# Seven-product pairs ordered by PSUM banks, a plain first part of six tiles, and features combined on VectorE

## The chip, the cores and the metric

The kernel runs on one core of a Trainium2 chip. The metric is the device time of one execution in microseconds (us). Comparisons use the median of several executions; the profile shows a single one. In the text PE is TensorE (matmuls), ACT is ScalarE, DVE is VectorE, POOL is GpSimd, and SP is the engine whose queue issues the loads of the weights.

## The reference

The kernel computes two layers of a hybrid decoder trunk on a sequence of 512 positions with 1024 features, all in float32. A layer is a feed-forward network (FFN), a mixer and a second FFN:

```python
def swiglu(h, w_gate, w_up, w_down):
    return (jax.nn.silu(h @ w_gate) * (h @ w_up)) @ w_down

for l in range(DEPTH):                                    # DEPTH = 2
    x = x + 0.5 * swiglu(rms_norm(x, ffn1_norm[l]), ffn1_w_gate[l], ffn1_w_up[l], ffn1_w_down[l])
    h = rms_norm(x, mix_norm[l])
    a, g, q, k, v = jnp.split(h @ w_in[l], splits, axis=-1)
    conv_out = conv_module(a, g, ...)                     # causal depthwise convolution, width 31
    diff_out = diff_attention(q, k, v, ...)               # 4 heads, two softmax maps each
    x = x + jnp.concatenate([conv_out, diff_out], axis=-1) @ w_out[l]
    x = x + 0.5 * swiglu(rms_norm(x, ffn2_norm[l]), ffn2_w_gate[l], ffn2_w_up[l], ffn2_w_down[l])
```

The hidden width of an FFN, D_FF, is 2816: 22 tiles of 128. There are four FFNs in all, and the change touches only them.

## The kernel before

**Layout.** Everything is kept transposed, with features on the 128 partitions and the 512 positions along the free dimension. `x` is 8 tiles of 128 x 512.

**Splitting.** A matmul operand in float32 is split into two operands of the type float32r: a high part (`hi`, a copy made by ACT) and a low part (`lo`, the remainder, subtracted by DVE). This is `parts_of`, lines 96 and 97. A product of two such operands takes three matmuls (high x high, high x low, low x high: `mm3`, lines 156, 159 and 160). `chunk` loads 128 x 1024 weights by a DMA on SP into a buffer of the ring `wraw` (6 buffers) and splits them into the rings `whi` and `wlo` (4 buffers each). `gather` (line 108) does the same for blocks of the down weights, and `whi2`, `wlo2` (2 buffers of 512) hold one more half tile.

**An FFN.** `ffn` runs over the 22 hidden tiles in three parts, `PARTS`, of 8, 8 and 6. In a part, each hidden tile is a *pair*: the gate product and the up product, 128 x 512 each, in two PSUM banks that `pair_banks` takes in turn from three tags (sc, po, mm). `gated` then splits silu(gate) * up into `hh` (ACT, line 374) and `hl` (DVE, line 375). When the tiles of a part are there, the down product runs: 8 output tiles, each a chain over the tiles of the part in a bank of the tag mm (`ps_d`), added to `x` by DVE (line 417).

**Plain pairs.** The first three pairs of an FFN (`PLAIN` = 3) are multiplied plainly, 2 x 8 x 3 = 48 matmuls of 512 columns. They use `x` times the gain, without the factor 1/rms, which is applied to their results. `first_products` makes the first two and the norm `r` (the tile `rb`) beside them.

**Seven-product pairs.** All later pairs use a scheme that has 7 products where 8 are usual: the input is cut in 2 x 2 blocks (first and second half of the features, first and second half of the positions), the weights in gate and up by halves of the features. The seven block products are 4 x 3 matmuls of 256 columns each, 84 in all. They need sums of weights (`sums`, line 123: two loads on SP, four additions on POOL, lines 136 to 140, and six splits) and combined features. `Halves` makes the latter once per FFN: `hn` is the normalised input (DVE, line 300), `ht` holds three differences of blocks (POOL, lines 303 and 304, and DVE, lines 305 and 306), which are split into `th` and `tl` (lines 307 and 308). `settle` then overwrites `acth` and `actl`, which the plain pairs read, with the split `hn` (lines 313 and 314).

**The order within a pair.** `seven` (line 323) accumulates in four half banks: a and d in the first bank, b and c in the second. A half bank that is wanted later in two places is copied by ACT to the tiles `g` and `n`. The framework takes a whole bank as the unit of waiting: PE does not write a bank while ACT or DVE reads it.

```python
go(a, "g1", "b11", first=True)
S.activation(g[:, :HS], a, AF.Copy)
go(c, "u2u1", "t1", first=True)
S.activation(n[:, HS:], c, AF.Copy)
go(b, "g2", "b21")
go(a, "g1u2u1", "t2")
S.activation(g[:, HS:], a, AF.Copy)
go(d, "u2", "t4")
...
go(a, "g1u1", "t3")
```

**What sets the order on the engines.** Each engine works its queue in order. The queues are filled by a scheduler that runs the program in a timeline of its own and gives each engine, of the instructions that are ready, the one that comes first in the program. The first matmul of each block product is pinned to the program's order. So matmuls of a down product may be put ahead of the last products of a part, and sums and splits of later weights run ahead as far as the rings have free buffers.

Of the kernel before, what the change touches and what calls it, by code (L numbers as in the profile page):

```python
# [37 lines left out]
MASK = -1e30  # L38
RLEN = 640
STATS_AT = 5  # L40

PLAIN = 3

PARTS = ((0, 8), (8, 8), (16, 6))
HS = SEQ // 2

SPACE = 392

# [18 lines left out]
def trunk(ctx: ExitStack, tc: tile.TileContext, xt, par, lamv, relb, onehot,  # L67
          gu1, dn1, wag, wqkv, wout, gu2, dn2, out):
    nc = tc.nc
    V, S, G, T = nc.vector, nc.scalar, nc.gpsimd, nc.tensor  # L70
# [4 lines left out]
    wp = ctx.enter_context(tc.tile_pool(name="wp", bufs=1))  # L75
# [78 lines left out]
    def mm3(ps, w, x, start, stop, pin=False):  # L154
        (wh, wl), (xh, xl) = w, x
        first = T.matmul(ps, wh, xh, start=start, stop=False)  # L156
# [29 lines left out]
    def col(l, name, i=0):  # L186
        c = _AT[name] + i
        return pars[l][:, c : c + 1]
# [91 lines left out]
    def pair_banks(turn):  # L280
        tag = ("sc", "po", "mm")[turn % 3]
        return [bank(tag, "ps_pair") for _ in range(2)]


    class Halves:
# [4 lines left out]
        def __init__(self, fp, pr, r):  # L290
            self.th = fp.tile([P, 3, KT // 2, HS], F32R, tag="th", name="th")
            self.tl = fp.tile([P, 3, KT // 2, HS], F32R, tag="tl", name="tl")

            self.whole = []
            free = [f"hh{n}" for n in range(PLAIN, 8)] + [f"hl{n}" for n in range(PLAIN, 6)]
            a, b = slice(0, HS), slice(HS, SEQ)
            for j in range(KT // 2):
                ha, hb = (fp.tile([P, SEQ], F32, tag=free[i], name="hn") for i in (2 * j, 2 * j + 1))
                for k, h in ((j, ha), (j + KT // 2, hb)):
                    V.scalar_tensor_tensor(h, x[:, k, :], col(pr.l, pr.gain, k), r, op0=ALU.mult, op1=ALU.mult)  # L300
                    self.whole.append((k, h))
                t = fp.tile([P, 3 + j % 2, HS], F32, tag=("ht", "hl6")[j % 2], name="ht")[:, :3]
                G.tensor_tensor(t[:, 1], hb[:, b], ha[:, b], op=ALU.subtract)
                G.tensor_tensor(ha[:, b], ha[:, a], ha[:, b], op=ALU.subtract)
                V.scalar_tensor_tensor(t[:, 0], ha[:, b], -1.0, hb[:, b], op0=ALU.mult, op1=ALU.subtract)
                V.scalar_tensor_tensor(t[:, 2], t[:, 0], -1.0, hb[:, a], op0=ALU.mult, op1=ALU.subtract)
                S.activation(self.th[:, :, j, :], t, AF.Copy)
                V.tensor_tensor(self.tl[:, :, j, :], t, f32(self.th[:, :, j, :]), op=ALU.subtract)
# [11 lines left out]
            k0, c = {"b11": (0, 0), "t1": (0, HS), "b21": (KT // 2, 0), "b22": (KT // 2, HS)}[name]  # L320
            return lambda j: (acth[:, k0 + j, c : c + HS], actl[:, k0 + j, c : c + HS])

    def seven(halves, w, banks, fp):

        a, d = banks[0][:, :HS], banks[0][:, HS:]
        b, c = banks[1][:, :HS], banks[1][:, HS:]
        g = fp.tile([P, SEQ], F32, tag="g", name="g", bufs=2)
        n = fp.tile([P, SEQ], F32, tag="n", name="n", bufs=2)

        def go(ps, wt, xt, first=False):  # L330


            at = halves.get(xt)
            for j in range(KT // 2):
                (wh, wl), (xh, xl) = wpart(w[wt], j), at(j)
                for i, (l, r) in enumerate(((wh, xh), (wh, xl), (wl, xh))):
                    mm = T.matmul(ps, l, r, start=first and i == j == 0, stop=False, skip_group_check=True)  # L337
                    if i == j == 0:
                        tc.keep_in_program_order(mm)

        go(a, "g1", "b11", first=True)
        S.activation(g[:, :HS], a, AF.Copy)
        go(c, "u2u1", "t1", first=True)
        S.activation(n[:, HS:], c, AF.Copy)  # L344
        go(b, "g2", "b21")
        go(a, "g1u2u1", "t2")
        S.activation(g[:, HS:], a, AF.Copy)  # L347
        go(d, "u2", "t4")
        S.activation(n[:, :HS], d, AF.Copy)
        go(c, "all", "b22")  # L350
        V.tensor_tensor(banks[1], banks[1], g, op=ALU.add)
        S.activation(g, banks[1], AF.Silu)
        go(a, "g1u1", "t3")
        V.tensor_tensor(d, a, n[:, HS:], op=ALU.add)
        V.tensor_tensor(a, a, n[:, :HS], op=ALU.add)
        V.scalar_tensor_tensor(banks[0], banks[0], -1.0, g, op0=ALU.mult, op1=ALU.mult)
        return banks[0]

    def ffn(pr, gu, dn, after, lead=None, aside=None):
        with tc.tile_pool(name="ffn", bufs=1) as fp:  # L360
            r = halves = None
            for m0, many in PARTS:
                hh, held, more = [], [], []

                def gated(n, us):
                    hi = fp.tile([P, SEQ], F32R, tag=f"hh{n}", name="hh")
                    if n < 6:
                        lo = fp.tile([P, SEQ], F32R, tag=f"hl{n}", name="hl")
                    elif n == 6:
                        two = fp.tile([P, 2, SEQ], F32R, tag="hl6", name="hl")  # L370
                        lo, more[:] = two[:, 0], [two[:, 1]]
                    else:
                        lo = more.pop()
                    S.activation(hi, us, AF.Copy)  # L374
                    V.tensor_tensor(lo, us, f32(hi), op=ALU.subtract)  # L375
                    hh.append((hi, lo))

                for mm in range(many):
                    m = m0 + mm
                    if m == 4 and aside:  # L380
                        aside()
                    if m >= PLAIN:
                        gated(mm, seven(halves, sums(gu[m, 0], gu[m, 1]), pair_banks(m), fp))
                        continue
                    w = lead if lead and m == 0 else [chunk(gu[m, 0]), chunk(gu[m, 1])]
                    held.append((mm, w, pair_banks(m)))
                    if m == 0:
                        continue
                    if m == 1:
                        _, _, r = first_products(pr, [h[1] for h in held], [h[2] for h in held])  # L390
                        halves = Halves(fp, pr, r)
                    else:
                        for k in range(KT):
                            for i in range(2):
                                mm3(held[-1][2][i], wpart(w[i], k), pr[k], k == 0, k == KT - 1)
                    if m == PLAIN - 1:
                        halves.settle()
                    for n, _, ps in held:
                        gs = fp.tile([P, SEQ], F32, tag="g", name="gs", bufs=2)
                        V.tensor_tensor(gs, ps[0], r, op=ALU.mult)  # L400
                        S.activation(gs, gs, AF.Silu)
                        us = fp.tile([P, SEQ], F32, tag="n", name="us", bufs=2)
                        V.tensor_tensor(us, ps[1], r, op=ALU.mult)
                        V.tensor_tensor(us, us, gs, op=ALU.mult)
# [363 lines left out]
    pr = Prep(0, "ffn1_norm")  # L768
# [7 lines left out]
    for l in range(DEPTH):  # L776
# [15 lines left out]
        pr = nxt["p"]  # L792
# [74 lines left out]
```

## Time and profile before

| | |
|---|---|
| time, median of 3 executions | 2130.51 us (2130.44 to 2132.23) |
| the profiled execution | 2129.2 us, of which its instructions span 2127.4 us |
| mean granted TensorE clock | 0.964 of full speed |
| busy: PE, weight loads, DVE, ACT, POOL | 87%, 76%, 63%, 44%, 39% of the span |
| HBM read | 172.74 MB, mean 83 GB/s over the span |

The page of the profile and the answers to questions on the trace give one execution. A row of a stretch lists, for each engine, its busy time and in brackets its instructions; then the granted clock, the mean busy share of the DMA engines and the rate. A row of waits says who waited for whom, then the sum in us, the times and the longest. A row of a group gives line, engine, operation, the written and read tiles with their shapes and the count, then the busy time, the mean of one in ns, and the idle time of the engine ahead of it with what ended it. A row of the timeline gives start, duration, and in square brackets the idle time before. Ends of matmuls are modelled, so a matmul's duration overlaps the next one; the distance of their starts is what one costs.

### The profile page before, as it was taken

The numbers are of one execution on the slowest core, as the hardware profiler recorded it, in microseconds if no ns is written. First come the engines' busy times: TensorE is split into PE (matmuls) and PEld (weight loads), VectorE is DVE, ScalarE is ACT, GpSimd is POOL, SyncE is SP. The second block draws the span as 40 slices with busy tenths as digits, with TensorE's granted clock in tenths as the row PEclk, the third lists the DMA queues.
The fourth block names the chain that finished last, engine by engine and source line by source line (L and its number), as shares of the span: only waits on it lengthen the run. The fifth ranks groups of instructions, "written<-read, shape, count | busy, mean of one in ns | idle before, by whom it ended". The sixth has DMA issues, their size and how long they took to land. (4 is left out here: it accounts for less than half of the span.)

```text
span 2127.4 us, 28881 instructions
## 1 busy us (share of the span) xinstructions
PE 1857.6 (87%) x11124; PEld 1625.7 (76%) x11124; DVE 1338.9 (63%) x1880; ACT 934.5 (44%) x1608; POOL 839.5 (39%) x576
## 2 busy tenths in 40 slices
PE   7589899899998598898986988989999958988988
PEld 5478788788787578878876788788887847788787
DVE  8655755558869655646576456465688686465463
ACT  5343533445745434424443334244458434244241
POOL 6313513139935414324044143240597452242330
PEclk9699999999999799999997999999999989999999
DMA  4232232332211131322411313224231213223131
GB/s 153 80 110 70 80 111 68 110 99 90 79 41 50 50 119 60 111 79 70 129 44 50 115 60 114 75 70 129 90 90 50 60 40 100 70 80 110 59 107 52
DMA packets 69017, 176.72 MB, mean 83 GB/s; under 512 B 8455, under 2 KB 26022, under 8 KB 68880
## 3 DMA queue, kind: packets, MB, share of 16 engines
q1 hardware_dynamic: 67104, 172.00, 25.3%
q0 software_dynamic: 1632, 2.81, 0.4%
q8 instruction: 87, 1.43, 0.3%
q14 instruction: 50, 0.41, 0.1%
q10 hardware_dynamic: 144, 0.08, 0.0%
HBM read 172.74 MB, written 3.42 MB: 83 GB/s over the span
## 5 line engine op out<-in xcount | busy, mean ns | idle before, releaser
L97 DVE TENSOR_TENSOR wlo<-wraw,whi 128x512 fp32r<-128x512 f32 (+1 forms) x582 | 612.2, 1082 | 283.5 <-ACT whi L96 281.0
L96 ACT ACTIVATE whi<-wraw 128x512 fp32r<-128x512 f32 (+1 forms) x626 | 478.1, 791 | 626.3 <-PE ps_pair L337 271.2
L136 POOL TENSOR_TENSOR wraw<-wraw 128x512 f32<-128x512 f32 x76 | 119.3, 1570 | 855.8 <-DMA wraw<-in_gu 544.2
L337 PE MATMUL ps_pair<-acth,whi 128*128 128x256 f32 x1216 | 356.1, 293 | 105.6 <-ACT acth L313 67.9
L337 PE MATMUL ps_pair<-actl,whi 128*128 128x256 f32 x1216 | 351.4, 289 | 13.6 <-DVE actl L314 13.6
L337 PE MATMUL ps_pair<-acth,wlo 128*128 128x256 f32 x1216 | 349.0, 287 | 0.4 <-DVE wlo L97 0.4
L337 PE MATMUL ps_pair<-th,whi 128*128 128x256 f32 x912 | 265.7, 292 | 93.9 <-ACT g L347 91.4
L337 PEld LDWEIGHTS ps_pair<-acth,whi 128*128 128x128 f32 x1216 | 237.6, 196 | 121.9 <-ACT acth L313 68.8
L156 PE MATMUL ps_d<-hh,whi 128*128 128x512 f32 x704 | 280.0, 401 | 31.8 <-ACT hh L374 29.9
L159 PE MATMUL ps_d<-hl,whi 128*128 128x512 f32 x704 | 280.7, 399 | 3.7 <-DVE hl L375 3.6
L160 PE MATMUL ps_d<-hh,wlo 128*128 128x512 f32 x704 | 280.5, 399 | 0.0
L337 PE MATMUL ps_pair<-tl,whi 128*128 128x256 f32 x912 | 259.1, 284 | 0.0
L337 PE MATMUL ps_pair<-th,wlo 128*128 128x256 f32 x912 | 258.8, 284 | 0.0
L337 PEld LDWEIGHTS ps_pair<-th,whi 128*128 128x128 f32 x912 | 175.5, 193 | 107.5 <-ACT g L347 104.2
L337 PEld LDWEIGHTS ps_pair<-actl,whi 128*128 128x128 f32 x1216 | 238.0, 196 | 18.6 <-DVE actl L314 17.8
L337 PEld LDWEIGHTS ps_pair<-acth,wlo 128*128 128x128 f32 x1216 | 238.2, 196 | 0.7 <-DVE wlo L97 0.7
L156 PEld LDWEIGHTS ps_d<-hh,whi 128*128 128x128 f32 x704 | 133.7, 191 | 66.6 <-ACT hh L374 32.4
L337 PEld LDWEIGHTS ps_pair<-tl,whi 128*128 128x128 f32 x912 | 176.0, 193 | 0.5
L337 PEld LDWEIGHTS ps_pair<-th,wlo 128*128 128x128 f32 x912 | 175.9, 193 | 0.0
L417 DVE SCALAR_TENSOR_TENSOR x<-ps_d,x 128x512 f32<-128x512 f32 x96 | 66.1, 690 | 168.5 <-PE ps_d L160 168.4
L159 PEld LDWEIGHTS ps_d<-hl,whi 128*128 128x128 f32 x704 | 135.8, 193 | 36.3 <-DVE hl L375 9.4
L160 PEld LDWEIGHTS ps_d<-hh,wlo 128*128 128x128 f32 x704 | 135.2, 192 | 31.0 <-DVE wlo L97 2.8
(177 smaller groups left out, 3325.7 us busy)
## 6 DMA issues: line engine op xcount, KB each, us to landing
wraw<-in_gu SPq DMA_DIRECT2D x174, 512.0 KB, 3.6
wraw<-in_wqkv SPq DMA_DIRECT2D x24, 512.0 KB, 3.6
wraw<-in_dn SPq DMA_DIRECT2D x52, 192.0 KB, 2.6
wraw<-in_wag SPq DMA_DIRECT2D x16, 512.0 KB, 3.5
wraw<-in_wout SPq DMA_DIRECT2D x16, 512.0 KB, 3.5
wraw<-in_dn SPq DMA_DIRECT2D x24, 320.0 KB, 3.2
wraw<-in_dn SPq DMA_DIRECT2D x28, 256.0 KB, 3.1
wraw<-in_dn SPq DMA_DIRECT2D x48, 128.0 KB, 3.3
```

Source lines behind the costliest of these rows:

```text
L96: S.activation(hi, raw, AF.Copy)
L97: (eng or V).tensor_tensor(out=lo, in0=raw, in1=f32(hi), op=ALU.subtract)
L136: G.tensor_tensor(two[:, h[1]], up[:, h[1]], up[:, h[0]], op=ALU.add)
L156: first = T.matmul(ps, wh, xh, start=start, stop=False)
L159: T.matmul(ps, wh, xl, start=False, stop=False)
L160: T.matmul(ps, wl, xh, start=False, stop=stop)
L337: mm = T.matmul(ps, l, r, start=first and i == j == 0, stop=False, skip_group_check=True)
L417: V.scalar_tensor_tensor(x[:, m, :], ps, 0.5, x[:, m, :], op0=ALU.mult, op1=ALU.add)
```

## The change

1. `PARTS` becomes 6, 8, 8 instead of 8, 8, 6, and `PLAIN` is the size of the first part: pairs 0 to 5 of each FFN are plain, 6 to 21 by seven products (before: 0 to 2 and 3 to 21). A plain pair finishes its gate product before its up product begins.
2. `Halves` is made after the first two pairs have been gated; both differences that POOL made are now made by DVE. Its `hn` tiles lie in `hh6`, `hh7`, `hl6`, `hl7` and the four buffers of `whi2` and `wlo2`. `settle` is called after the pairs of the first part, ahead of its down product.
3. `seven` has another order of products: c, d, [the last product of the pair before], a, b, c, a. Its own last product (g1 + u1 with t3) and the steps that follow it are returned as a function `rest`, which the next pair calls in its third place, or `finish` at the end of a part. In the last pair of a part, the fifth and sixth products change places. The copies go to one tile `keep` of four half rows; a and d are copied by one instruction.
4. The tiles `g` and `n` become one tile of the tag `gn`; the special case for `hl6` goes.

`sums` itself is the same in both kernels: its four additions were on POOL already.

```diff
-PLAIN = 3
-PARTS = ((0, 8), (8, 8), (16, 6))
+PARTS = ((0, 6), (6, 8), (14, 8))
+PLAIN = PARTS[0][1]
...
-            free = [f"hh{n}" for n in range(PLAIN, 8)] + [f"hl{n}" for n in range(PLAIN, 6)]
+            free = [(fp, tag, 1) for tag in ("hh6", "hh7", "hl6", "hl7")]
+            free += [(wp, tag, 2) for tag in ("whi2", "wlo2") for _ in range(2)]
...
-                G.tensor_tensor(t[:, 1], hb[:, b], ha[:, b], op=ALU.subtract)
-                G.tensor_tensor(ha[:, b], ha[:, a], ha[:, b], op=ALU.subtract)
+                V.tensor_tensor(t[:, 1], hb[:, b], ha[:, b], op=ALU.subtract)
+                V.tensor_tensor(ha[:, b], ha[:, a], ha[:, b], op=ALU.subtract)
...
-    def seven(halves, w, banks, fp):
+    def seven(halves, w, banks, fp, before, last):
...
-        go(a, "g1", "b11", first=True)
-        S.activation(g[:, :HS], a, AF.Copy)
         go(c, "u2u1", "t1", first=True)
-        S.activation(n[:, HS:], c, AF.Copy)
+        S.activation(keep[:, 3], c, AF.Copy)
+        go(d, "u2", "t4", first=True)
+        before()
+        go(a, "g1", "b11")
+        S.activation(keep[:, :2], banks[0].rearrange("p (n c) -> p n c", n=2), AF.Copy)
         go(b, "g2", "b21")
+        if not last:
+            go(c, "all", "b22")
         go(a, "g1u2u1", "t2")
-        S.activation(g[:, HS:], a, AF.Copy)
-        go(d, "u2", "t4")
-        S.activation(n[:, :HS], d, AF.Copy)
-        go(c, "all", "b22")
-        V.tensor_tensor(banks[1], banks[1], g, op=ALU.add)
-        S.activation(g, banks[1], AF.Silu)
-        go(a, "g1u1", "t3")
-        V.tensor_tensor(d, a, n[:, HS:], op=ALU.add)
-        V.tensor_tensor(a, a, n[:, :HS], op=ALU.add)
-        V.scalar_tensor_tensor(banks[0], banks[0], -1.0, g, op0=ALU.mult, op1=ALU.mult)
-        return banks[0]
+        S.activation(keep[:, 2], a, AF.Copy)
+        if last:
+            go(c, "all", "b22")
+        V.tensor_tensor(two, two, g, op=ALU.add)
+        S.activation(g, two, AF.Silu)
+
+        def rest():
+            go(a, "g1u1", "t3")
+            V.tensor_tensor(d, a, keep[:, 3], op=ALU.add)
+            V.tensor_tensor(a, a, keep[:, 1], op=ALU.add)
+            us = banks[0].rearrange("p (n c) -> p n c", n=2)
+            V.scalar_tensor_tensor(us, us, -1.0, g, op0=ALU.mult, op1=ALU.mult)
+            return banks[0]
+
+        return rest
...
+                def finish():
+                    if late:
+                        n, rest = late.pop()
+                        gated(n, rest())
...
                     if m >= PLAIN:
-                        gated(mm, seven(halves, sums(gu[m, 0], gu[m, 1]), pair_banks(m), fp))
+                        w = sums(gu[m, 0], gu[m, 1])
+                        late.append((mm, seven(halves, w, pair_banks(m), fp, finish, mm == many - 1)))
                         continue
...
-                        for k in range(KT):
-                            for i in range(2):
-                                mm3(held[-1][2][i], wpart(w[i], k), pr[k], k == 0, k == KT - 1)
-                    if m == PLAIN - 1:
-                        halves.settle()
+                        for i in range(2):
+                            products(pr, w, held[-1][2][i], i)
...
+                    if m == 1:
+                        halves = Halves(fp, pr, r)
+                finish()
+                if m0 == 0:
+                    halves.settle()
```

More of the change, by code (lines that the diff above doesn't have):

```diff
@@ L294, in __init__ @@
             self.whole = []
-            free = [f"hh{n}" for n in range(PLAIN, 8)] + [f"hl{n}" for n in range(PLAIN, 6)]
+            free = [(fp, tag, 1) for tag in ("hh6", "hh7", "hl6", "hl7")]
+            free += [(wp, tag, 2) for tag in ("whi2", "wlo2") for _ in range(2)]
             a, b = slice(0, HS), slice(HS, SEQ)
             for j in range(KT // 2):
-                ha, hb = (fp.tile([P, SEQ], F32, tag=free[i], name="hn") for i in (2 * j, 2 * j + 1))
-                for k, h in ((j, ha), (j + KT // 2, hb)):
+                for k in (j, j + KT // 2):
+                    pool, tag, bufs = free.pop()
+                    h = pool.tile([P, SEQ], F32, tag=tag, name="hn", bufs=bufs)
                     V.scalar_tensor_tensor(h, x[:, k, :], col(pr.l, pr.gain, k), r, op0=ALU.mult, op1=ALU.mult)
                     self.whole.append((k, h))
-                t = fp.tile([P, 3 + j % 2, HS], F32, tag=("ht", "hl6")[j % 2], name="ht")[:, :3]
-                G.tensor_tensor(t[:, 1], hb[:, b], ha[:, b], op=ALU.subtract)
-                G.tensor_tensor(ha[:, b], ha[:, a], ha[:, b], op=ALU.subtract)
+                (_, ha), (_, hb) = self.whole[-2:]
+                t = fp.tile([P, 3, HS], F32, tag="ht", name="ht", bufs=2)
+                V.tensor_tensor(t[:, 1], hb[:, b], ha[:, b], op=ALU.subtract)
+                V.tensor_tensor(ha[:, b], ha[:, a], ha[:, b], op=ALU.subtract)
                 V.scalar_tensor_tensor(t[:, 0], ha[:, b], -1.0, hb[:, b], op0=ALU.mult, op1=ALU.subtract)
@@ L321, in get @@
             return lambda j: (acth[:, k0 + j, c : c + HS], actl[:, k0 + j, c : c + HS])
-    def seven(halves, w, banks, fp):
+    def seven(halves, w, banks, fp, before, last):
         a, d = banks[0][:, :HS], banks[0][:, HS:]
         b, c = banks[1][:, :HS], banks[1][:, HS:]
-        g = fp.tile([P, SEQ], F32, tag="g", name="g", bufs=2)
-        n = fp.tile([P, SEQ], F32, tag="n", name="n", bufs=2)
+        two = banks[1].rearrange("p (n c) -> p n c", n=2)
+        keep = fp.tile([P, 4, HS], F32, tag="gn", name="keep", bufs=2)
+        g = keep[:, 0::2]
         def go(ps, wt, xt, first=False):
@@ L362, in ffn @@
             for m0, many in PARTS:
-                hh, held, more = [], [], []
+                hh, held, late = [], [], []
                 def gated(n, us):
                     hi = fp.tile([P, SEQ], F32R, tag=f"hh{n}", name="hh")
[L367 to L373, printed above, removed]
+                    lo = fp.tile([P, SEQ], F32R, tag=f"hl{n}", name="hl")
                     S.activation(hi, us, AF.Copy)
```

11 lines of the change are left out of this document (5 added, 6 removed).

## The prediction

> **What bounds the kernel now.** I read the page first, then the time by stretch, then who made TensorE (PE) wait, then the chain of waits and single instructions where it pointed.
>
> ```profile
> span 2127.4 us, 28881 instructions
> PE 1857.6 (87%) x11124; PEld 1625.7 (76%) x11124; DVE 1338.9 (63%) x1880; ACT 934.5 (44%) x1608; POOL 839.5 (39%) x576
> ```
>
> PE is the busiest. The stretches, with PE's instructions in brackets behind its busy time and the granted clock after POOL; those with a clock under 1 are the starts of the four feed-forward networks (FFN):
>
> ```profile
> core 0: us, PE busy (x) PEld busy (x) DVE busy (x) ACT busy (x) POOL busy (x), PEclk, DMA share, GB/s
> 629.00:648.00 19.00, 19.00 (x161) 19.00 (x160) 11.22 (x18) 8.15 (x14) 4.65 (x3) 1.00 0.18 58
> 1077.00:1084.00 7.00, 7.00 (x32) 5.79 (x32) 3.33 (x2) 1.25 (x2) 5.64 (x4) 1.00 0.26 75
> 46.40:158.80 112.40, 73.83 (x469) 66.51 (x467) 66.96 (x98) 45.93 (x80) 27.13 (x25) 0.80 0.28 90
> 685.30:782.40 97.10, 65.66 (x463) 60.52 (x462) 57.60 (x84) 42.78 (x75) 23.99 (x16) 0.88 0.24 76
> 1108.10:1205.90 97.80, 67.86 (x464) 62.70 (x462) 57.19 (x81) 40.37 (x71) 21.45 (x16) 0.86 0.24 76
> 1732.80:1829.90 97.10, 65.67 (x463) 60.51 (x462) 58.62 (x84) 42.79 (x75) 22.20 (x16) 0.88 0.24 76
> 1865.30:1975.40 110.10, 94.14 (x715) 89.04 (x714) 67.75 (x85) 51.14 (x93) 35.57 (x24) 1.00 0.29 92
> 1872.50:1947.50 75.00, 63.49 (x504) 61.05 (x504) 52.69 (x67) 38.43 (x73) 30.60 (x20) 1.00 0.30 99
> 2013.20:2095.40 82.20, 70.09 (x536) 66.60 (x534) 48.04 (x63) 38.31 (x69) 24.36 (x16) 1.00 0.24 78
> ```
>
> The first two rows are stretches in which PE never rests: 256-column matmuls start every 19.00/160 = 0.119 us, 512-column ones every 7.00/31 = 0.226. A pair by seven products (84 x 256) so needs 10.0 us, a plain pair (48 x 512) 10.85. The row 1872.50 holds exactly six seven-pairs (504 matmuls) in 75.0 us: 12.5 each, 2.5 lost per pair, at full clock. Who made PE wait:
>
> ```profile
> PE ps_pair L337 <- ACT g L347: 91.4, 63, 1.7
> PE ps_pair L337 <- ACT acth L313: 67.9, 4, 18.1
> PE ps_pair L337 <- ACT n L344: 35.7, 63, 6.1
> PE ps_d L156 <- ACT hh L374: 29.9, 12, 2.5
> ```
>
> The first and third are the copies out of a PSUM bank in which PE wants to go on; in the chain of waits they recur each 12.5 us, with a weight split ahead of the copy in ACT's queue:
>
> ```profile
> 1884.98 0.61 ACT whi L96
> 1885.92 7.46 PE ps_pair L337 x60
> 1893.84 3.02 PE ps_pair L337 x23
> 1897.48 0.61 ACT whi L96
> ```
>
> The second happens once per FFN. The timeline shows PE at a standstill for 18 us between the plain and the seven-product pairs, because the features (L304) stand in POOL's queue behind a sum of weights that waits for a load:
>
> ```profile
> 1743.92 3.57 POOL L136 TENSOR_TENSOR wraw<-wraw 128x512 f32<-128x512 f32 x1 [13.19 <-DMA wraw<-in_gu]
> 1753.38 1.40 POOL L304 TENSOR_TENSOR hn<-hn 128x256 f32<-128x256 f32 x2
> 1754.82 0.58 PE L337 MATMUL ps_pair<-acth,whi 128*128 128x256 f32 x1 [18.05 <-ACT acth L313]
> 1732.80:1761.00 28.20, 6.34 (x25) 4.82 (x24) 21.18 (x34) 12.71 (x21) 10.87 (x8) 0.58 0.07 19
> ```
>
> In the last row 25 matmuls (3 us) take 28.2 us, at a mean clock of 0.58.
>
> **The lost time, stage by stage.** A first part holds 5 seven-pairs (420 x 256) and 42 early down matmuls: 50.0 + 9.5 = 59.5 us. It took 97.1, 97.8 and 97.1: 37.6, 38.3 and 37.6 lost; 112.4 in the first FFN, 52.9 lost (it also prepares the bias). The second part (672 x 256, 42 x 512: 89.5) took 110.1: 20.6 lost; the third (504, 30: 66.8) took 82.2: 15.4. I take these two for all four FFNs. In all 166.4 + 82.4 + 61.6 = 310.4 us. Without it the kernel would take 2127.4 - 310.4 = 1817.0.
>
> **Plain part of six.** Twelve pairs go from seven-product to plain: 12 x 0.85 = +10.2 us of PE, so 1827.2 is the floor. Their loads on SP stay two of 512 KB a pair; 48 sums leave POOL. The down weights are still 22 gathers an FFN (6, 8, 8 instead of 8, 8, 6), on SP ahead of the loads for pair 6.
>
> **Halves and settle.** Features can now be made under pairs 2 to 5 (43.4 us of PE), and `settle` (8 copies on ACT, 8 subtractions on DVE) runs under the first down product, 144 x 0.226 = 32.5 us. So the 28 us hole should go, and the low clock with it. What comes late next is DVE:
>
> ```profile
> 1721.00:1733.00 12.00, 12.00 (x54) 9.78 (x53) 11.99 (x13) 4.49 (x7) 6.87 (x6) 1.00 0.15 44
> 1724.63 7.31 DVE L300 SCALAR_TENSOR_TENSOR hn<-x,par,rb 128x512 f32<-128x512 f32 x8
> L308 DVE TENSOR_TENSOR tl<-ht,th 128x768 fp32r<-128x768 f32 x16 | 16.7, 1056 | 0.7 <-ACT th L307 0.6
> 1829.17 1.22 DVE L97 TENSOR_TENSOR wlo<-wraw,whi 128x1024 fp32r<-128x1024 f32 x1
> ```
>
> DVE is full when the norm becomes known. From there to the end of pair 5 it has features: 7.3 + 4 x (1.06 + 4 x 0.43, 256-wide steps as in the row of L355 below) = 18.4, of which the two steps taken from POOL are 8 x 0.43 = 3.4; six pairs to gate, four steps of 0.68 each: 16.3; and eight weight splits of 1.22: 9.8. That is 44.5 us of work for about 43 of PE. The features stand ahead of the splits of pairs 3 and 4, so a split will be late: between 0 and 8 us an FFN. I take 4, since the later pairs' splits can slide under PE's own time: +16 in all.
>
> **Seven products by banks.** The steps of the six pairs in the row 1872.50, and some of them alone:
>
> ```profile
> L97 DVE TENSOR_TENSOR wlo<-wraw,whi 128x512 fp32r<-128x512 f32 x31 | 26.3, 893 | 15.4 <-ACT whi L96 15.4
> L97 DVE TENSOR_TENSOR wlo<-wraw,whi 128x1024 fp32r<-128x1024 f32 x6 | 10.2, 1700 | 0.0
> L356 DVE SCALAR_TENSOR_TENSOR ps_pair<-ps_pair,g 128x512 f32<-128x512 f32 x6 | 4.2, 700 | 0.6
> L375 DVE TENSOR_TENSOR hl<-ps_pair,hh 128x512 fp32r<-128x512 f32 x6 | 4.1, 680 | 0.0
> L355 DVE TENSOR_TENSOR ps_pair<-ps_pair,n 128x256 f32<-128x256 f32 x6 | 2.6, 432 | 0.2
> L96 ACT ACTIVATE whi<-wraw 128x1024 fp32r<-128x1024 f32 x6 | 6.4, 1058 | 0.0
> L352 ACT ACTIVATE g<-ps_pair 128x512 f32<-128x512 f32 x6 | 3.6, 599 | 8.7 <-DVE ps_pair L351 8.7
> L349 ACT ACTIVATE n<-ps_pair 128x256 f32<-128x256 f32 x6 | 2.2, 367 | 0.0
> 1913.21 0.69 DVE L97 TENSOR_TENSOR wlo<-wraw,whi 128x512 fp32r<-128x512 f32 x1 [0.85 <-ACT whi L96]
> 1917.23 2.18 DVE L97 TENSOR_TENSOR wlo<-wraw,whi 128x1024 fp32r<-128x1024 f32 x1
> 1917.03 1.30 POOL L136 TENSOR_TENSOR wraw<-wraw 128x512 f32<-128x512 f32 x1 [6.43 <-DMA wraw<-in_gu]
> 1918.29 2.28 POOL L137 TENSOR_TENSOR wraw<-wraw 128x512 f32<-128x512 f32 x1
> ```
>
> Now two products in other banks (one, in the last pair of a part) lie between a copy's start and PE's next use of that bank, 2 x 12 x 0.119 = 2.9 us against copies of 0.37 to 0.60, so the waits on L344 and L347 go. Moved into the next pair are 12 matmuls, three DVE steps and the split of the gated tile, and no load. Behind the moved product on PE stands the rest of the next pair; its sums of weights keep their slot a third of a pair longer. The wait that is next late is the first product's weights: their slot comes free when the fourth group of a pair ends (g2 x b21), 24 matmuls or 2.9 us ahead of use, in which ACT splits (0.61) and DVE subtracts. Whether that holds hangs on DVE's load per pair: 5 x 0.89 + 1.70 + 2 x 0.70 + 0.68 + 2 x 0.43 = 9.1 us of the 10.0; ACT has 38.43/6 = 6.4, POOL 30.60/5 = 6.1. So everything fits, DVE barely. A split that meets a sum on POOL takes 2.18 instead of 1.22, and the sum 2.28 instead of 1.30. I expect 0.5 us of PE waiting per pair (bounds 0 and 1.5, a little over one such meeting of 0.96): 64 x 0.5 = +32.
>
> **Smaller terms.** The 2.5 us waits for the last gated tile (29.9 in twelve) shrink, as early down matmuls now have few other holes to fill: +8 kept. In part three the first product wants the bank of the last down chain (turn 14 takes the tag mm, second bank first): one evacuation of about 0.7 and its start, +4 in all. The bias preparation of the first FFN: +5.
>
> Sum: 1827.2 + 16 + 32 + 8 + 4 + 5 = 1892. The profiled execution of before took 2129.2 us, 1.8 over its span, and the median is 1.3 above that: **1895 us**.
>
> **Rivals.** *The shared path of DVE and POOL paces the pairs.* If every split met a sum, the split work would grow by 2.18/1.22 = 1.79: uncontended 5 x 0.69 + 1.22 = 4.67 becomes 8.3, plus 2.9 of DVE work from PSUM: 11.3 us per pair. 64 x 1.3 = 83 in place of 32: 1946. For it speaks that both slow down when they meet; against it that a shorter pair leaves POOL its PSUM-side gaps (2.9 us) to work in. The Trainium skill, SBUF — State Buffer, section Who interferes with whom, says that a DVE operation with two SBUF inputs and a GpSimd operation reading SBUF exclude each other, the second blocking fully; by that rule 4.67 and 4 x 1.30 of sums would fill 9.9 of the 10.0 us, which speaks against this change. The trace agrees that both are lengthened where they meet (2.18 and 2.28 above).
>
> *The stalls only change place.* If each pair still loses its 2.5 us to some copy or split, 64 x 2.5 = 160 replaces 32: 2023. The change would then not do what it says. Against it: the two named waits have lost their cause.
>
> *Slower: the weights of the next pair's first product.* Should ACT and DVE split them only behind the gate sum, its Silu and the whole-tile split of the next pair (0.70 + 0.60 + 1.06 + 1.70 + 0.61 + 0.89), PE waits 5.6 us at each pair's start: 64 x 5.6 = 358, 2221. It decides from 4.2 us per pair on, (2127 - 1827 - 33)/64. For it: the splits ahead of the copies in the chain above are just such an order. Against: the slot is free 2.9 us early and the engines have room.
>
> **How the numbers follow.** Forecast (a pair below 10.9 us) 0.66; shared path 0.19; moved stalls 0.08; slower 0.05; a time as before 0.01; less waiting than I allow, under 1850, 0.01. The own range of the forecast is 1850 to 1925; with the shared path and late splits (8 per FFN, +16) it reaches to 1985, leaving out the last cases. A measurement here tells 0.2% (4 us) from no change: faster 0.94, within 0.01, slower 0.05.
>
> **What would show it.** Right: the stretch of a second part holds seven-pairs every 10 to 10.9 us; no wait on the copies of the pairs above 10 us in sum; no PE wait on `settle`; clock 1.00 at the start of part two; DVE near 90% in that stretch. A late-split step shows as PE waits on whi or wlo in pairs 3 and 4. Wrong: a wait on whi or wlo at every pair's start, or a DVE stretch at 100% with pairs above 11 us.

## The result and the profile after

The changed kernel takes 1860.56 us (median of 4, 1859.78 to 1861.82) against 2130.48 for the kernel before on the same chips: 0.8732 of the time, interval 0.8717 to 0.8747. That is faster, as forecast, 34 us under the predicted 1895 and inside the range of 1850 to 1985. The profiled execution took 1859.78 us, its span is 1858.0, and the mean granted clock rose from 0.964 to 0.997.

The head of the page of the changed kernel:

```profile
span 1858.0 us, 27488 instructions
PE 1805.1 (97%) x10692; PEld 1585.3 (85%) x10692; DVE 1320.6 (71%) x1852; ACT 877.5 (47%) x1450; POOL 758.7 (41%) x496
```

PE has gone from 87% to 97% of the span. DVE, ACT and POOL do a little less than before (POOL a tenth less) in 269 us less. The stretches, in the columns used before (length, PE with its count, PEld, DVE, ACT, POOL, clock, DMA share, GB/s):

```profile
80.00:126.60 46.60, 35.37 (x147) 27.87 (x146) 24.34 (x30) 13.10 (x21) 12.73 (x10) 0.89 0.26 85
1516.00:1562.00 46.00, 46.00 (x204) 38.12 (x203) 39.66 (x60) 22.81 (x32) 3.04 (x2) 1.00 0.30 91
1562.00:1597.40 35.40, 33.81 (x146) 26.72 (x144) 21.24 (x26) 9.15 (x14) 10.42 (x8) 1.00 0.20 60
1597.40:1686.30 88.90, 86.66 (x694) 84.79 (x693) 71.03 (x81) 47.01 (x83) 37.93 (x24) 1.00 0.37 113
1607.40:1667.10 59.70, 57.46 (x470) 56.45 (x470) 53.63 (x61) 32.80 (x60) 32.85 (x20) 1.00 0.33 101
1725.70:1814.40 88.70, 86.64 (x694) 84.75 (x693) 70.01 (x81) 47.05 (x83) 39.08 (x24) 1.00 0.36 108
```

The first row is the first down product of the first FFN, at a clock of 0.89. The second is the plain part of the last FFN, the third its down product with `settle` beside it, the fourth and sixth its two parts of eight seven-pairs, the fifth a piece of the second part. The standstill of 18 us that stood ahead of the seven-pairs is gone: PE is busy for all 46.00 us of the second row, at full clock, in the place where 28.2 us ran at 0.58. Who made PE wait, in the changed kernel:

```profile
PE ps_pair L343 <- DVE wlo L97: 17.6, 33, 0.7
PE ps_d L156 <- DVE gs L413: 11.7, 4, 10.5
PE ps_d L156 <- ACT hh L382: 3.0, 4, 0.9
```

The copies, 127.1 us before, no longer stand in the list; `acth` with its 67.9 is gone too. The new first row is the low part of the first product's weights, 0.53 us each time. The second lies almost wholly in one place of the first FFN. The third had 29.9.

The timeline of one steady pair shows where the first row comes from (start, duration, engine, line, operation, in brackets the idle time before):

```profile
1620.52 0.69 DVE L360 TENSOR_TENSOR ps_pair<-ps_pair,keep 128x512 f32<-128x512 f32 x1
1624.56 4.60 DVE L97 TENSOR_TENSOR wlo<-wraw,whi 128x512 fp32r<-128x512 f32 x3
1625.16 1.74 POOL L137 TENSOR_TENSOR wraw<-wraw 128x512 f32<-128x512 f32 x1
1626.87 1.74 POOL L139 TENSOR_TENSOR wraw<-wraw 128x512 f32<-128x512 f32 x1
1631.38 0.69 DVE L360 TENSOR_TENSOR ps_pair<-ps_pair,keep 128x512 f32<-128x512 f32 x1
1634.51 0.63 ACT L96 ACTIVATE whi<-wraw 128x512 fp32r<-128x512 f32 x1 [0.86 <-DMA wraw<-in_gu]
1635.43 4.59 DVE L97 TENSOR_TENSOR wlo<-wraw,whi 128x512 fp32r<-128x512 f32 x3
1638.37 0.39 PE L343 MATMUL ps_pair<-acth,wlo 128*128 128x256 f32 x1 [0.53 <-DVE wlo L97]
```

The same step of two pairs (L360) lies 31.38 - 20.52 = 10.86 us apart. In each pair three weight splits stand in a row on DVE: that of a later pair's `u2`, which ACT begins when its load has landed (1634.51), then the two of the buffer that the next pair's first product reads (`u2u1`, and with it `g1u2u1`). They take 1.53 us each in the mean, while sums on POOL run at the same time. PE then waits 0.53 us for the second of them.

### The profile page after: what moved, and what is told of

It is laid out like the page before. It is cut to its first block, busy times and chain, and to the rows that moved or that the text cites. A ratio compares the mean times of both kernels' runs of the same rounds, so it can differ in the third digit from the quotient of the medians.

```text
span 1858.0 us, 27488 instructions
## 1 busy us (share of the span) xinstructions
PE 1805.1 (97%) x10692; PEld 1585.3 (85%) x10692; DVE 1320.6 (71%) x1852; ACT 877.5 (47%) x1450; POOL 758.7 (41%) x496
## 4 chain that ended last, share of the span: by engine, by line
PE 76%; DVE 17%; ACT 3%; issue 3%; DMA 2%; SPq 0%; POOL 0%; DVEq 0%; ACTq 0%; POOLq 0%
PE ps_pair L343 21%; DVE wlo L97 11%; PE ps_d L156 8%; PE ps_d L159 8%; PE ps_d L160 8%; PE ps_pair L159 5%; PE ps_pair L160 5%; PE ps_pair L156 5%; ACT whi L96 2%; PE ps_pair L550 2%; PE ps_pair L551 2%; PE ps_pair L549 2%; PE ps_out L159 1%; PE ps_out L156 1%; PE ps_sc L667 1%
## 5 line engine op out<-in xcount | busy, mean ns | idle before, releaser
L343 PE MATMUL ps_pair<-acth,wlo 128*128 128x256 f32 x1024 | 293.7, 287 | 17.7 <-DVE wlo L97 17.6
L343 PE MATMUL ps_pair<-acth,whi 128*128 128x256 f32 x1024 | 289.6, 283 | 0.0
L343 PE MATMUL ps_pair<-actl,whi 128*128 128x256 f32 x1024 | 289.5, 283 | 0.0
L343 PEld LDWEIGHTS ps_pair<-acth,wlo 128*128 128x128 f32 x1024 | 196.1, 192 | 25.6 <-DVE wlo L97 25.6
L343 PE MATMUL ps_pair<-th,whi 128*128 128x256 f32 x768 | 217.3, 283 | 0.0
L343 PE MATMUL ps_pair<-tl,whi 128*128 128x256 f32 x768 | 217.2, 283 | 0.0
L156 PE MATMUL ps_pair<-acth,whi 128*128 128x512 f32 x512 | 200.2, 394 | 5.5 <-ACT whi L96 5.5
L159 PE MATMUL ps_pair<-actl,whi 128*128 128x512 f32 x512 | 201.0, 393 | 2.0 <-DVE actl L242 1.7
L160 PE MATMUL ps_pair<-acth,wlo 128*128 128x512 f32 x512 | 200.4, 392 | 0.6 <-DVE wlo L97 0.6
L343 PEld LDWEIGHTS ps_pair<-actl,whi 128*128 128x128 f32 x1024 | 196.3, 192 | 0.3
L159 PEld LDWEIGHTS ps_d<-hl,whi 128*128 128x128 f32 x704 | 132.7, 188 | 28.2 <-DVE hl L383 1.7
```

## The experiments

My theory at this point: the order by banks and the plain part each remove their own loss (the copies, the hole), and what is left in the pairs comes from DVE splits that meet POOL sums. The rival for the pairs was that the moved product, or the order of the queue alone, costs the time; for the size of the gain, that one of the two parts does all the work. Ratios are to the kernel before.

**The order alone.** The kernel before, with the new `seven`, `rest` and `finish`; `PARTS`, `PLAIN`, `Halves` and `settle` stay as they were.

```diff
-                        gated(mm, seven(halves, sums(gu[m, 0], gu[m, 1]), pair_banks(m), fp))
+                        w = sums(gu[m, 0], gu[m, 1])
+                        late.append((mm, seven(halves, w, pair_banks(m), fp, finish, mm == many - 1)))
```

> The kernel before with the new order of the seven products alone (last product in the next pair, copies into one tile); parts of 8, 8, 6, three plain pairs, features on POOL and settle ahead of the first seven-product pair as before. Theory (two separate gains: banks in the pairs, and the hole at the start of the seven-product pairs): a pair falls from 12.5 to about 10.5 us, so 76 x 2 = 152 us go and most of the twelve waits of 2.5 us at the ends of the parts: 1950 to 1980 us, and the hole of about 25 us with the low clock stays in each FFN. Rival (the order helps only because the plain part has freed the engines): above 2050 us. Rival (the order is all): below 1900 us.

Measured: 1950.74 us, 0.9163 (0.9147 to 0.9179), clock 0.974. The waits of PE:

```profile
PE ps_pair L340 <- ACT acth L313: 67.8, 4, 17.5
PE ps_pair L340 <- DVE wlo L97: 15.0, 29, 0.7
PE ps_pair L340 <- ACT keep L349: 4.2, 2, 3.2
```

Of the waits on copies 4.2 us are left, the hole of some 17 us an FFN stands as it was, and the 0.5 us waits on `wlo` are there already. So those waits come with the order and not with the plain part.

**The plain part alone.** The changed kernel with the old `seven`.

```diff
-                        w = sums(gu[m, 0], gu[m, 1])
-                        late.append((mm, seven(halves, w, pair_banks(m), fp, finish, mm == many - 1)))
+                        gated(mm, seven(halves, sums(gu[m, 0], gu[m, 1]), pair_banks(m), fp))
```

> The changed kernel with the old order of the seven products and their old copies; the plain first part of six, the features on VectorE and settle under the first down product stay. Theory: the hole at the start of the seven-product pairs is gone (about 27 us an FFN, more in the first), the pairs stay at 12.5 us: 1860 + 64 x 2.1 + about 20 for the ends of the parts = 2000 to 2025 us, and the waits of TensorE on the two copies return. Rival (the plain part also relieves the copies, through emptier queues): below 1960 us.

Measured: 2006.34 us, 0.9422 (0.9405 to 0.9438). Waits, then a stretch in a part of seven-pairs:

```profile
PE ps_pair L340 <- ACT keep L350: 81.6, 56, 1.7
PE ps_pair L340 <- ACT keep L347: 26.5, 56, 0.5
```

```profile
1707.90:1798.30 90.40, 76.92 (x613) 74.04 (x612) 60.37 (x77) 45.82 (x85) 34.58 (x24) 1.00 0.30 94
```

Here the hole is gone and the copies are back: 612 matmuls take 90.4 us instead of 72.8. The two edits remove what was put down to each. Alone they save 180 and 124 us, together 270, 34 less than the sum. Twelve pairs that the plain part takes out of the seven-product scheme also lose their 2.5 us by the new order, and 12 x 2.5 = 30 is counted in both; that is worked out, not measured by itself.

**The last product in its own pair.** No product is moved into the next pair; all pairs use the order of a last one.

```diff
-                        late.append((mm, seven(halves, w, pair_banks(m), fp, finish, mm == many - 1)))
+                        late.append((mm, seven(halves, w, pair_banks(m), fp, lambda: None, True)))
+                        finish()
```

> The changed kernel in which each pair ends with its own last product: the order that the last pair of a part has is used in all pairs, nothing is moved into the next pair. Theory (what counts is that a product in another bank lies between a copy and the next use of its bank, and one product, 1.4 us, is enough): 1850 to 1870 us. The slot of the next pair's first weights would even come free 4.3 instead of 2.9 us ahead. Rival (ScalarE's queue makes a copy wait for weight splits, so that one product is too short): TensorE waits 0.5 to 1 us more per pair on the copies, 1890 to 1925 us.

Measured: 1871.49 us, 0.879 (0.8775 to 0.8805): 11 us slower than the change, between the two expectations. In the pairs it is a little quicker: most of them are 10.35 us apart, where the change has 10.86. PE's matmuls behind a copy, and the wait that grew:

```profile
1635.64 0.28 PE L343 MATMUL ps_pair<-acth,wlo 128*128 128x256 f32 x1
1635.93 0.39 PE L343 MATMUL ps_pair<-th,whi 128*128 128x256 f32 x1
1636.15 0.28 PE L343 MATMUL ps_pair<-tl,whi 128*128 128x256 f32 x1
```

```profile
PE ps_d L156 <- ACT hh L382: 14.7, 12, 1.5
```

The starts lie 0.29 and 0.22 us apart instead of 0.12, some 0.27 us a pair; there is no wait on `wlo` in the pairs. The time is lost at the ends of the parts: 14.7 us of waits for the last gated tile in place of 3.0. The move into the next pair so pays where the down product begins, not in the pairs. That it makes the first weights late is not shown by this run alone, for the order without it also frees their buffer earlier.

**Features back on POOL.** The two differences of `Halves`.

```diff
-                V.tensor_tensor(t[:, 1], hb[:, b], ha[:, b], op=ALU.subtract)
-                V.tensor_tensor(ha[:, b], ha[:, a], ha[:, b], op=ALU.subtract)
+                G.tensor_tensor(t[:, 1], hb[:, b], ha[:, b], op=ALU.subtract)
+                G.tensor_tensor(ha[:, b], ha[:, a], ha[:, b], op=ALU.subtract)
```

> The changed kernel with the two differences of features on GpSimd again. Theory (the hole came from the place of the features behind sums that wait for loads, and the plain part takes the sums away): GpSimd is idle in the plain part, 1857 to 1864 us, no change that shows. Rival (it was the engine): the wait ahead of the seven-product pairs returns in part, 10 us or more an FFN, above 1900 us.

Measured: 1861.75 us, 0.8744 (0.8725 to 0.8763), no difference from the change. With hardly a sum in the plain part (3.04 us of POOL in the 46.00 above) POOL has room, and DVE has too. With six plain pairs it does not matter which engine makes the differences. Whether DVE alone would have closed the hole with three plain pairs was not tried.

**The sums left out.** POOL's four additions shrink to two of 16 columns, and four splits read the loads themselves instead of sums. The splits, their number and their queue stay. It computes other products than the reference.

```diff
-        G.tensor_tensor(two[:, h[1]], up[:, h[1]], up[:, h[0]], op=ALU.add)
-        G.tensor_tensor(two[:, h[0]], whole[:, h[0]], up[:, h[0]], op=ALU.add)
-        G.tensor_tensor(more[:, h[0]], two[:, h[1]], whole[:, h[0]], op=ALU.add)
-        G.tensor_tensor(more[:, h[1]], more[:, h[0]], whole[:, h[1]], op=ALU.add)
+        e = slice(0, 16)
+        G.tensor_tensor(two[:, e], up[:, e], whole[:, e], op=ALU.add)
+        G.tensor_tensor(more[:, e], two[:, e], whole[:, e], op=ALU.add)
...
```

> The changed kernel whose four sums of weights on GpSimd are made on 16 columns only; the splits take the loaded weights in place of the sums, so the products are of other numbers (left out: the sums). All splits, loads, products and waits for buffers stay. Theory (a split that meets a sum on GpSimd is lengthened, and so the first product of a pair waits for its low part): splits of 512 columns fall from 1.25 to about 0.69 us, the waits on the low parts (0.5 to 0.7 us a pair) go: 1828 to 1840 us. Rival (the buffer comes free too late whatever the split takes): 1852 us or more, the waits stay.

Measured: 1823.15 us, 0.8558 (0.8546 to 0.8571), a little below the theory. The splits as a group in the changed kernel (the stretch 1607.4 to 1667.1), then without sums (1590 to 1650), and a stretch of the latter:

```profile
L97 DVE TENSOR_TENSOR wlo<-wraw,whi 128x512 fp32r<-128x512 f32 x27 | 32.6, 1254 | 1.6 <-ACT whi L96 1.6
```

```profile
L97 DVE TENSOR_TENSOR wlo<-wraw,whi 128x512 fp32r<-128x512 f32 x24 | 15.7, 690 | 11.9 <-ACT whi L96 11.9
1555.00:1640.00 85.00, 85.00 (x662) 82.89 (x662) 52.84 (x80) 45.30 (x80) 4.93 (x12) 1.00 0.28 92
```

A split takes 690 ns instead of 1254, DVE waits for ACT instead of being nearly full, and PE has no gap left. The wait on `wlo` in the pairs is gone from the list. Leaving out the sums also spares the splits a wait for them, but that wait is not what bound: the two late splits behind 1635.43 above read sums that POOL had finished before 1629. So the meeting with the sums is a cause of the late splits.

**The moved product two places later.** `before()` between g2 x b21 and the rest, to give the first weights more time.

```diff
         go(d, "u2", "t4", first=True)
-        before()
...
         go(b, "g2", "b21")
+        before()
```

> The changed kernel with the last product of the pair before two places later: after the second product of the gate (c, d, a, b, [last of the pair before], c, a). The buffer of the next pair's first weights then comes free 36 matmuls, 4.3 us, ahead of their use instead of 2.9. Theory (the lead is what the lengthened split lacks): the waits on the low parts go, 0.5 to 0.7 us for most of 64 pairs: 1825 to 1840 us. Rival (VectorE's load per pair sets the pace, 90% busy): the wait turns up elsewhere, 1852 to 1865 us.

Measured: 1938.54 us, 0.9103 (0.9089 to 0.9117), clock 0.982: a miss, 78 us slower than the change where theory and rival had 1825 to 1865.

```profile
PE ps_pair L343 <- DVE wlo L97: 69.1, 39, 2.8
```

```profile
191.95 2.62 ACT L96 ACTIVATE whi<-wraw 128x512 fp32r<-128x512 f32 x4 [1.42 <-DMA wraw<-in_gu]
192.62 3.53 DVE L97 TENSOR_TENSOR wlo<-wraw,whi 128x512 fp32r<-128x512 f32 x2 [2.61 <-ACT whi L96]
197.87 0.39 PE L343 MATMUL ps_pair<-acth,wlo 128*128 128x256 f32 x1 [2.65 <-DVE wlo L97]
```

ACT stands 1.42 us for a load: the first of the four splits in that row is that of a later pair's `u2`, whose weights were asked for at 188.2 and landed at 191.9, and those of the next pair's first products stand behind it. DVE waits 2.61 us for ACT, PE 2.65 for DVE. This is a reading of the queue; the last two runs test it.

**The mixer's scalars first.** In the bias preparation of the first FFN, DVE's queue waits for a small load that POOL issues behind a larger copy. In the changed kernel:

```profile
71.46 1.16 POOL L453 DMA_DIRECT2D d<-d  x1 [3.89 <-DMA d<-brow]
72.61 0.57 POOL L463 DMA_DIRECT2D lamv<-in_lamv  x1
88.15 0.23 DVE L465 TENSOR_TENSOR lamp<-lamv 128x64 f32<-128x64 f32 x1 [6.67 <-DMA lamv<-in_lamv]
94.20 0.79 PE L156 MATMUL ps_d<-hh,whi 128*128 128x512 f32 x1 [10.51 <-DVE gs L413]
```

```diff
-        make_bias()
         make_scalars()
+        make_bias()
```

> The changed kernel with the scalars of the mixer made ahead of the bias instead of behind it, so that their small loads stand ahead of the bias's 1280 KB copy in GpSimd's queue. Theory (in the first FFN the last plain pair waits because VectorE stands at a product of a load that lands 15 us late, and the bank of the first down chain with it): 8 to 11 us less, 1849 to 1853 us. Rival (VectorE is late from its own load in the plain part): 1858 to 1862 us, the 10.5 us wait stays.

Measured: 1846.53 us, 0.8669 (0.8656 to 0.8682), 14 us less than the change, more than the 8 to 11 expected.

```profile
80.00:115.60 35.60, 35.27 (x163) 29.20 (x162) 23.08 (x26) 10.40 (x15) 16.23 (x11) 1.00 0.34 111
```

The first down product now takes 35.6 us at full clock, as the other FFNs' do, in place of 46.6 at 0.89.

**Gate and up interleaved.** The plain pairs' old inner order, k outside.

```diff
-                        for i in range(2):
-                            products(pr, w, held[-1][2][i], i)
+                        for k in range(KT):
+                            for i in range(2):
+                                mm3(held[-1][2][i], wpart(w[i], k), pr[k], k == 0, k == KT - 1)
```

> The changed kernel whose plain pairs 2 to 5 run gate and up interleaved over the eight blocks of features, as before, instead of gate first. Theory (with gate first its result is evacuated under the up product, and the last pair's first bank, which the first down chain needs, is free at once): undone, TensorE waits 0.7 to 2 us more at the end of each first part: 1863 to 1870 us. Rival (hidden anyway): 1858 to 1862 us.

Measured: 1862.37 us, 0.8742 (0.8728 to 0.8757), no difference. Finishing the gate product early is hidden in any case.

**One buffer for `u2`.** On top of the scalars first, `whi2` and `wlo2` have one buffer each, so that a later `u2` can't be split until the present one is used. Two of the `hn` tiles get buffers of their own in exchange.

```diff
-    RING = {"wraw": 6, "whi": 4, "wlo": 4, "whi2": 2, "wlo2": 2}
+    RING = {"wraw": 6, "whi": 4, "wlo": 4, "whi2": 1, "wlo2": 1}
...
-            free = [(fp, tag, 1) for tag in ("hh6", "hh7", "hl6", "hl7")]
-            free += [(wp, tag, 2) for tag in ("whi2", "wlo2") for _ in range(2)]
+            free = [(fp, tag, 1) for tag in ("hh6", "hh7", "hl6", "hl7", "hx0", "hx1")]
+            free += [(wp, tag, 1) for tag in ("whi2", "wlo2")]
```

> The changed kernel with the scalars ahead of the bias (as in the run of that) and with one buffer instead of two for the split half tile u2; two of the eight normalised tiles get tiles of their own instead. So the split of u2 can't run two pairs ahead any more, just as its load lands and GpSimd begins its sums, in front of the splits for the next pair's first product. Theory (that place, and not the load of VectorE in sum, makes the first low part late): the waits on the low parts go, 1820 to 1830 us. Rival (VectorE and GpSimd together fill the pair): the waits stay or move, 1840 to 1850 us.

Measured: 1814.15 us, 0.8512 (0.8498 to 0.8527), the best of all, 32 us below the scalars first alone. A stretch of a part, and DVE in it:

```profile
1562.00:1638.30 76.30, 76.30 (x637) 76.28 (x636) 64.39 (x78) 44.98 (x79) 36.90 (x24) 1.00 0.36 112
1598.84 1.28 DVE L97 TENSOR_TENSOR wlo<-wraw,whi 128x512 fp32r<-128x512 f32 x2
1599.82 1.47 POOL L136 TENSOR_TENSOR wraw<-wraw 128x512 f32<-128x512 f32 x1 [3.98 <-DMA wraw<-in_gu]
1601.69 3.10 DVE L97 TENSOR_TENSOR wlo<-wraw,whi 128x512 fp32r<-128x512 f32 x2 [0.97 <-ACT whi L96]
```

PE rests nowhere in 76 us. The two splits for the next pair's first product (1598.84) no longer stand behind one that waits for a load. They are done in 1.28 us, before that load sets off the sums (1599.82). The two that still meet sums (1601.69, 3.10 us) belong to products late in the pair. So the late split needs both: the `u2` split ahead of it, which holds it back until the sums run, and the sums, which lengthen it. Either one taken away frees the pairs.

**One buffer, and the moved product later.** The two edits joined, with the scalars first.

```diff
-    RING = {"wraw": 6, "whi": 4, "wlo": 4, "whi2": 2, "wlo2": 2}
+    RING = {"wraw": 6, "whi": 4, "wlo": 4, "whi2": 1, "wlo2": 1}
...
         go(d, "u2", "t4", first=True)
-        before()
...
         go(b, "g2", "b21")
+        before()
```

> As the run with one buffer for u2, and with the last product of the pair before two places later (c, d, a, b, [last of the pair before], c, a). Theory (the later place cost 78 us because ScalarE's split of u2, which waited for a load, stood ahead of the first weights' split; with one buffer it doesn't): 1815 to 1835 us, no wait of 2.7 us at the pairs' starts. Rival (the later place itself is bad, for the steps of VectorE behind it come too close to the next pair): above 1880 us.

Measured: 1819.94 us, 0.8551 (0.853 to 0.8572).

```profile
PE ps_pair L343 <- DVE wlo L97: 1.4, 6, 0.4
```

The 69.1 us of waits fall to 1.4. So the early `u2` split did the damage, as the reading of ACT's queue had it, and not the later place. The later place gains nothing either: it is 6 us slower than one buffer alone.

## Why the prediction was right, step by step

**The two losses and the floor.** Right in mechanism. The run with the order alone and the run with the plain part alone each remove the loss they were charged with. Of the 65 us that I kept above the floor of 1827.2, the span shows 30.8. The floor itself is a little low: 637 starts of 256-column matmuls in 76.30 us without a gap are 76.30/636 = 0.120 us apart, where I had 0.119; over 64 x 84 matmuls that is 5 us.

**Late splits in the plain part, +16.** Mis-sized: 0 measured. No wait lies in the 46 us of that part. I had DVE with 44.5 us of work for 43; it did 39.66 in 46.00, 86%. Putting the two differences back on POOL, which empties DVE a little, changes nothing either.

**Half a microsecond per pair, +32, and the part ends, +8.** The eight stretches of eight seven-pairs took 88.5 to 89.5 us, 710.95 in all. Each needs 672 x 0.119 + 21 x 0.226 = 84.7, so 33.4 us are lost over 64 pairs, part ends included, where I had 40; 5 of them are the pitch just named. The cause is the one that I named, a split that meets sums; its place in the queue, behind a third split, I had not seen. It is also less even than "0.5 each": 33 pairs waited, and a pair with such a wait takes 10.86 us instead of 84 x 0.120 = 10.08, so they alone make 33 x 0.78 = 26. The waits for the last gated tile fell to 3.0, under the 8 kept.

**The bank of the last down chain, +4.** Nothing to be seen: third parts took as long as second ones, 88.7 and 88.9 in the rows above.

**The bias preparation, +5.** Mis-sized: 11.2, from 46.6 against 35.4 us for the first down product. I had taken the whole excess loss of the first FFN's first part as gone but for 5. A part of it was a wait that neither edit touches. In the kernel before, DVE stands 7.4 us for the same small load `lamv`, ACT's queue stands behind DVE, and PE waits 6.1 us for the copy that comes next on ACT: that is the longest wait in the row of L344 that I showed, and I read it as a matter of copies. In the changed kernel the load costs 10.5 us.

**The remainder.** The terms as measured give 1827.2 + 33.4 + 11.2 = 1871.8, and the span is 13.8 shorter. I had left all other stretches at their old lengths. That put at nothing the low clock behind the twelve 2.5 us waits for the last gated tile. In the kernel before, eight of them are followed by a stretch at half clock in the down product behind, seven of 3.4 us and one of 6.8. Two of these down products of before, and the successor of the second of them:

```profile
159.00:195.00 36.00, 35.64 (x149) 28.57 (x149) 18.11 (x20) 8.65 (x11) 12.50 (x8) 0.95 0.25 73
1975.40:2013.20 37.80, 37.42 (x150) 30.05 (x151) 17.87 (x20) 8.58 (x11) 12.52 (x9) 0.91 0.22 70
```

```profile
1686.30:1725.70 39.40, 39.07 (x173) 32.05 (x172) 18.34 (x23) 10.21 (x14) 12.80 (x9) 1.00 0.21 67
```

In the second row 150 x 0.226 = 33.9 us of matmuls took 37.8 at a clock of 0.91; now 173 x 0.226 = 39.1 take 39.4. The eight stretches are 30.7 us at half clock, which cost some 15 us of PE's time (an estimate: half of them). The changed kernel has none of them, and that is about the 13.8. The other runs agree: with the plain part alone the waits for the last gated tile stay (23.0 us) and five are followed by half clock; with the order alone they are 1.5 us at most and none is.

**The rivals.** The shared path of DVE and POOL did not pace the pairs: at 11.3 us it would have left DVE no gap, and pairs took mostly 10.86, 11.2 at worst, and 10.08 with one buffer for `u2`. But its mechanism, together with the order of the queue, makes most of the 33.4 us. The rule of the Trainium skill (SBUF — State Buffer, section Who interferes with whom) is that a DVE operation with two SBUF inputs and a GpSimd operation that reads SBUF contend for a shared port pair, which it calls an exclusive lock; that the second is blocked fully it says of the 2-port modes. The traces agree that both get slower, and nearly with the total of an exclusion: see the last section. By exclusion 9.9 us of a pair would be filled, and that fitted into the 10.08. The stalls did not simply change place, and the weights of the next pair's first product were late by 0.53 us and not by 5.6; the run with the later place shows, though, that an order of this kind can come about: with one far load at the head of ACT's queue PE waited up to 2.8 us a time, 69.1 in all. The upper end of the range, 1985, is not added up in the prediction: the shared path with late splits is 1946 + 16 = 1962.

**What would show it.** Pairs at 10 to 10.9 us, no wait on the copies or on `settle`, full clock at the start of the second part, and DVE at 53.63/59.7 = 90% in its steady piece: all seen, but for a few pairs of up to 11.2. Splits late in pairs 3 and 4: not seen.

## What to carry to other kernels

When an accumulator bank is both read and wanted again, put other banks' products in between before looking for faster copies: that took away 127 us of waits here. A ring with one buffer more isn't free: it lets work for a far pair be queued in order ahead of work that is wanted next, and one buffer instead of two was worth 32 us. Before a loss is written off with the hole that it stands near, look in the trace for waits of other causes in it (6.1 us here, and 10.5 afterwards). And look at the granted clock behind short waits: their cost did not end with them (some 15 us here).

## What the runs showed of the hardware that was not expected

A weight split of 512 columns takes 0.69 us alone and 1.78 when sums run on POOL all the while (1.53 in the mean of the rows above); a sum takes 1.26 alone and 1.74 then. The records of both engines lengthen. In the 4.60 us of the row at 1624.56, three splits (2.07 alone) pass beside two whole sums (2.5 alone) and the ends of two more, 0.6 and 0.5 us of their records. One after the other that would be some 5.4 us (an estimate from the durations alone), so the total is near to an exclusion, but below it. Whether one operation blocks the other as a whole is not shown.

```profile
90.33 1.26 POOL L137 TENSOR_TENSOR wraw<-wraw 128x512 f32<-128x512 f32 x1
```

The clock falls after short waits, but not after each. With the moved product later, PE waits 2.65 us, and then runs at half clock for 6.6 us:

```profile
171.92 0.58 PE L343 MATMUL ps_pair<-acth,wlo 128*128 128x256 f32 x1 [2.65 <-DVE wlo L97]
171.90:178.50 6.60, 6.58 (x32) 6.59 (x33) 5.08 (x7) 1.47 (x3) 1.09 (x1) 0.53 0.46 150
```

Thirty-two matmuls take 6.60 us there instead of 3.8, so the lost time doubles. This is the longest case. Of the 20 waits of 2.4 to 2.8 us on `wlo` in that run, 15 are followed by a stretch at half clock, the other 14 of these 3.4 us long, and five by none. Together they explain that run: 69.1 - 17.6 = 51.5 us of waits more, and half of 54.6 us at half clock, make 79 us, and it was 78 us slower. Waits of 1.4 to 1.5 us, such as those for the copy of L347 in the kernel before, are not followed by a lower clock. The Trainium skill, TensorE: Matmul & The Clock Gate, section What's actually happening, puts the fall behind an idle window of about 3.4 us; here 2.65 us of rest were enough.

A matmul that starts just when what it waits for is done pushes the pitch of its neighbours from 0.12 to 0.29 and 0.22 us, although hardly any idle time is recorded before it, as the rows of the run with the last product in its own pair show (there it waits for the copy of L357). Such starts cost there some 0.27 us a pair.
